# A 4096-cubed matmul on one core: the panel of B halved to 1024 columns and double-buffered, and the order of TensorE and of the loads written out by hand

## The chip, the cores and the metric

The kernel runs on one core of one Trainium2 chip. Times are device microseconds (us) of that core, from the start to the end of one execution; of several executions the median is given. The trace is of one profiled execution.

## The reference

```python
m, k, n = 4096, 4096, 4096
a = np.random.randn(m, k).astype(np.float32)
b = np.random.randn(k, n).astype(np.float32)
scale = np.float32(0.1)
out = np.matmul(a, b) * scale          # float32
```

The kernel multiplies in bf16 and sums in float32.

## The kernel before

All loads that change float32 into bf16 on the way (A and B) are issued by POOL, one DMA for 128 partitions x 512 columns: 256 KB are read from memory and 128 KB written to SBUF. All other DMAs (stores of the output, and the stores and loads of the transposed A) are issued by SP.

A comes in 32 row tiles `mt` of 128 rows. A is needed transposed, so `make_at` (lines 59 to 77) loads one row tile in eight DMAs into `arow_bf` (three buffers), transposes it on TensorE (PE) in 32 pieces into PSUM (line 72), and VectorE copies the result into `at` (line 73). Each `at` is also stored to a scratch tensor in memory, `at_dram` (line 75), from where `load_at` (lines 79 to 84) fetches it again for later columns.

B is held in SBUF by panels of `N_BLK` = 2048 columns: 32 slices of k (`ko`) times 4 column groups of 512, that is 128 tiles `bp` of 128 KB (line 119). The pool of `bp` has 136 slots (line 51). There are two panels, so two blocks `nb`: block 0 uses columns 0 to 2047 and makes every `at`; block 1 uses the other columns and loads every `at` again.

For one row tile, `matmuls` (lines 86 to 107) runs 128 matmuls of 128x128 by 128x512: two PSUM banks at a time, each of 32 steps of `ko` (line 93). ScalarE (ACT) multiplies the bank by the scale (line 103) and SP stores it (line 104).

The order of the instructions on each engine is set by the scheduler of the tile framework, with the order of the program as priority; each engine then runs its own queue in order. A DMA of POOL waits on its queue until the slot that it writes is free and until the DMA eight before it on the same queue has landed.

Of the kernel before, what the change touches and what calls it, by code (L numbers as in the profile page):

```python
# [1 line left out]

# [5 lines left out]

FP32 = mybir.dt.float32  # L10
BF16 = mybir.dt.bfloat16


@with_exitstack
def kernel(
    ctx: ExitStack,
    tc: tile.TileContext,
    a: bass.AP,
    b: bass.AP,
    scale: float,  # L20
    out: bass.AP,
):
    nc = tc.nc
    P = 128

    M, K = a.shape
    K2, N = b.shape
    assert K == K2

    N_BLK = 2048  # L30
    NT = 512
    KO = K // P
    MT = M // P
    PS_GRP = 2
    AROW_Q = 8
    AHEAD = 3

    n_blocks = N // N_BLK
    nts = N_BLK // NT

    b_r = b.rearrange("(ko ki) n -> ki ko n", ki=P)

    dram = ctx.enter_context(tc.tile_pool(name="dram", bufs=1, space=bass.MemoryType.DRAM))
    at_dram = dram.tile([MT, P, K], BF16)

    const_pool = ctx.enter_context(tc.tile_pool(name="const", bufs=1))
    ident = const_pool.tile([P, P], BF16)
    make_identity(nc, ident)

    arow_pool = ctx.enter_context(tc.tile_pool(name="arow", bufs=3))  # L50
    bp_pool = ctx.enter_context(tc.tile_pool(name="bp", bufs=KO * 4 + 8))
    at_pool = ctx.enter_context(tc.tile_pool(name="at", bufs=AHEAD + 1))
    cst_pool = ctx.enter_context(tc.tile_pool(name="cst", bufs=6))
    psum_pool = ctx.enter_context(tc.tile_pool(name="psum", bufs=2 * PS_GRP, space=bass.MemoryType.PSUM))
    psum_tr_pool = ctx.enter_context(tc.tile_pool(name="psum_tr", bufs=8 - 2 * PS_GRP, space=bass.MemoryType.PSUM))

    TRB = 8

    def make_at(mt):
        arow_bf = arow_pool.tile([P, K], BF16, tag="arow_bf")  # L60
        for q in range(AROW_Q):
            w = K // AROW_Q
            nc.gpsimd.dma_start(  # L63
                out=arow_bf[:, q * w:(q + 1) * w],
                in_=a[mt * P:(mt + 1) * P, q * w:(q + 1) * w],
            )
        at = at_pool.tile([P, KO, P], BF16, tag="at")
        for g in range(KO // TRB):
            ps_t = psum_tr_pool.tile([P, TRB, P], BF16, tag="pst", name="ps_t")
            for j in range(TRB):  # L70
                ko = g * TRB + j
                nc.tensor.transpose(ps_t[:, j], arow_bf[:, ko * P:(ko + 1) * P], ident)  # L72
            nc.vector.tensor_copy(out=at[:, g * TRB:(g + 1) * TRB, :], in_=ps_t)  # L73
        for q in range(2):
            nc.sync.dma_start(out=at_dram[mt, :, q * (K // 2):(q + 1) * (K // 2)],
                              in_=at[:, q * (KO // 2):(q + 1) * (KO // 2), :])
        return at

    def load_at(mt):
        at = at_pool.tile([P, KO, P], BF16, tag="at")  # L80
        for q in range(4):
            nc.sync.dma_start(out=at[:, q * (KO // 4):(q + 1) * (KO // 4), :],
                              in_=at_dram[mt, :, q * (K // 4):(q + 1) * (K // 4)])
        return at

    def matmuls(bp, at, mt, nb):
        for v in range(nts // PS_GRP):
            psums = [psum_pool.tile([P, NT], FP32, tag="ps", name="ps") for _ in range(PS_GRP)]
            for ko in range(KO):
                lhsT = at[:, ko, :]  # L90
                for g in range(PS_GRP):
                    nt = v * PS_GRP + g
                    nc.tensor.matmul(  # L93
                        psums[g],
                        lhsT,
                        bp[ko][nt],
                        start=(ko == 0),
                        stop=(ko == KO - 1),
                    )
            for g in range(PS_GRP):  # L100
                nt = v * PS_GRP + g
                cst = cst_pool.tile([P, NT], FP32, tag="cst")
                nc.scalar.mul(cst, psums[g], float(scale))  # L103
                nc.sync.dma_start(
                    out=out[mt * P:(mt + 1) * P, nb * N_BLK + nt * NT:nb * N_BLK + (nt + 1) * NT],
                    in_=cst,
                )

    at_q = []
    for nb in range(n_blocks):  # L110
        while len(at_q) < AHEAD:
            mt = len(at_q)
            at_q.append(make_at(mt) if nb == 0 else load_at(mt))

        bp = [[bp_pool.tile([P, NT], BF16, tag="bp", name="bp") for _ in range(nts)]
              for _ in range(KO)]
        for q in range(nts):
            for ko in range(KO):
                nc.gpsimd.dma_start(  # L119
                    out=bp[ko][q],  # L120
                    in_=b_r[:, ko, nb * N_BLK + q * NT:nb * N_BLK + (q + 1) * NT],
                )

        for mt in range(MT):
            at_cur = at_q.pop(0)
            if mt + AHEAD < MT:
                at_q.append(make_at(mt + AHEAD) if nb == 0 else load_at(mt + AHEAD))
            matmuls(bp, at_cur, mt, nb)
        at_q = []


# [1 line left out]
_INS = ['a', 'b', 'scale']  # L133
_OUTS = [((4096, 4096), 'float32')]
#: Inputs that are plain numbers.
_NUMBERS = {'scale': 0.10000000149011612}


# [26 lines left out]
```

## Time and profile before

| what | value |
|---|---|
| median of 4 runs | 1953.43 us (1952.56 to 1957.6) |
| the profiled execution's own time | 1957.6 us, the highest of the four |
| its span in the trace | 1955.8 us |
| PE busy | 1884.3 us, 96% of the span |
| matmuls on line 93 | 8192, of which 8017 have a record |
| transposes on line 72 | 1024 |
| mean granted clock of PE | 0.991 of full speed |
| mean DMA rate (bytes written) | 104 GB/s |

Ends of matmuls are modelled in this trace, so a busy PE isn't PE at its full rate; a few per cent of the matmul records are missing, while the weight loads (one for each matmul and each transpose, row PEld) are all there and count the work done. "Clock" is the clock of PE that was granted, 1.00 being 2.4 GHz and 0.50 being 1.2 GHz. "DMA share" is the busy time of the packets of the mean DMA engine over the stretch; packets of two queues overlap, so it goes above 1.

### The profile page before, as it was taken

What the parts mean: (1) busy time and instruction counts of PE and PEld (TensorE: products, weight loads), DVE (VectorE), ACT (ScalarE), POOL (GpSimd) and SP (SyncE); (2) the same over time, 40 slices, a digit from 0 to 9 for tenths busy, and PEclk for the clock granted to TensorE, in tenths of its full rate; (3) what the DMA queues carried; (4) which work ended last, traced back from release to release, by engine and by line L of the source; (5) the groups of instructions that cost most, each with busy time, mean ns of one, the idle gap of its engine ahead of it and who ended that gap; (6) DMA issues with size and microseconds to landing.
All of it is one profiled execution on the core that took longest, in us unless ns stands there. A gap on an engine that the chain in (4) does not pass through costs nothing.

```text
span 1955.8 us, 20456 instructions
## 1 busy us (share of the span) xinstructions
PE 1884.3 (96%) x9041; PEld 864.1 (44%) x9216; DVE 80.9 (4%) x128; ACT 140.5 (7%) x257; POOL 271.4 (14%) x518
## 2 busy tenths in 40 slices
PE   6889999999999999999996899999999999999999
PEld 2134444444444444444441344444444444444444
DVE  1011101101101101101000000000000000000000
ACT  0000000000000000000000000000000000000000
POOL 6762111111111111100036300000000000000000
PEclk9999999999999999999997999999999999999999
DMA  9997345345345345331269622222222122212201
GB/s 210 196 229 161 98 107 119 98 107 119 97 108 119 97 108 119 96 88 76 78 128 211 135 84 86 76 71 70 86 75 83 58 86 75 86 57 84 86 33 44
DMA packets 138328, 202.70 MB, mean 104 GB/s; under 512 B 15360, under 2 KB 80896, under 8 KB 138240
## 3 DMA queue, kind: packets, MB, share of 16 engines
q0 software_dynamic: 73728, 67.14, 22.5%
q1 hardware_dynamic: 64512, 134.25, 19.6%
q8 instruction: 72, 1.18, 0.3%
q14 instruction: 16, 0.13, 0.0%
HBM read 167.77 MB, written 100.66 MB: 137 GB/s over the span
## 4 chain that ended last, share of the span: by engine, by line
PE 88%; DMA 5%; issue 3%; POOL 3%; ACTq 0%; POOLq 0%; ACT 0%
PE ps L93 86%; DMA bp<-in_b_dram 4%; PE ps_t L72 3%; POOL bp L119 2%; DMA arow_bf<-in_a_dram 1%; POOL arow_bf L63 1%; ACTq L160 0%; POOL ident masks.py:199 0%; POOL ident masks.py:197 0%; ACT cst L103 0%; POOLq masks.py:199 0%; POOLq L119 0%; POOLq L160 0%; POOLq L146 0%
## 5 line engine op out<-in xcount | busy, mean ns | idle before, releaser
L93 PE MATMUL ps<-bp,at 128*128 128x512 bf16 x8017 | 1822.4, 383 | 49.3 <-DMA bp<-in_b_dram 31.7
L93 PEld LDWEIGHTS <-at 128*128 128x128 bf16 x8192 | 802.3, 98 | 1051.9 <-issue 103.3
L103 ACT ACTIVATE cst<-ps 128x512 f32<-128x512 f32 x256 | 139.2, 595 | 1811.4 <-issue 1658.4
L63 POOL DMA_DIRECT2D arow_bf<-in_a_dram x256 | 135.6, 560 | 597.8 <-PE ps_t L72 568.4
L119 POOL DMA_DIRECT2D bp<-in_b_dram x256 | 135.2, 532 | 225.6 <-PE ps L93 176.9
L73 DVE COPY at<-ps_t 128x1024 bf16<-128x1024 bf16 x128 | 80.9, 685 | 837.7 <-PE ps_t L72 837.7
L72 PE MATMUL ps_t<-ident,arow_bf 128*128 128x128 bf16 x1024 | 73.9, 229 | 18.1 <-DMA arow_bf<-in_a_dram 17.6
L72 PEld LDWEIGHTS <-arow_bf 128*128 128x128 bf16 x1024 | 63.6, 102 | 35.2 <-DMA arow_bf<-in_a_dram 28.0
L103 ACT ACT_TABLE_LOAD x1 | 1.3, 1283 | 0.7 <-PEq L146 0.7
masks.py:199 POOL TENSOR_SCALAR_AFFINE_SELECT ident<-ident 128x128 bf16<-128x128 bf16 x1 | 0.3, 304 | 0.1
masks.py:197 POOL MEMSET ident<- 128x128 bf16 x1 | 0.2, 204 | 0.3 <-POOLq L146 0.3
L146 POOL MEMSET const-float32-0.0<- 128x1 f32 x1 | 0.1, 99 | 0.2 <-issue 0.2
L146 POOL MEMSET const-bfloat16-1.0<- 128x1 bf16 x1 | 0.1, 102 | 0.0
L146 POOL MEMSET const-uint8-127<- 128x1 uint8 x1 | 0.1, 102 | 0.0
L146 POOL MEMSET const-float32-1.0<- 128x1 f32 x1 | 0.1, 99 | 0.0
## 6 DMA issues: line engine op xcount, KB each, us to landing
out_dram<-cst SPq DMA_DIRECT2D x256, 256.0 KB, 2.7
arow_bf<-in_a_dram POOLq DMA_DIRECT2D x256, 128.0 KB, 7.3
at_dram<-at SPq DMA_DIRECT2D x64, 512.0 KB, 6.3
bp<-in_b_dram POOLq DMA_DIRECT2D x256, 128.0 KB, 4.9
at<-at_dram SPq DMA_DIRECT2D x128, 256.0 KB, 5.0
```

Of the source, the lines that this page charges most:

```text
L63: nc.gpsimd.dma_start(out=arow_bf[:, q * w:(q + 1) * w], in_=a[mt * P:(mt + 1) * P, q * w:(q + 1) * w],)
L72: nc.tensor.transpose(ps_t[:, j], arow_bf[:, ko * P:(ko + 1) * P], ident)
L73: nc.vector.tensor_copy(out=at[:, g * TRB:(g + 1) * TRB, :], in_=ps_t)
L93: nc.tensor.matmul(psums[g], lhsT, bp[ko][nt], start=(ko == 0), stop=(ko == KO - 1),)
L103: nc.scalar.mul(cst, psums[g], float(scale))
L119: nc.gpsimd.dma_start(out=bp[ko][q], in_=b_r[:, ko, nb * N_BLK + q * NT:nb * N_BLK + (q + 1) * NT],)
L146: nc = _bacc.Bacc("TRN2", target_bir_lowering=False, num_devices=1)
```

## The change

A panel is 1024 columns wide, so there are four panels and four blocks; the pool of `bp` has 128 slots, two panels of 64. `make_at` now only issues the eight loads; the transposes, the copies and the stores to `at_dram` (now four DMAs of 256 KB where there were two of 512 KB) are in `transpose_at`. The queues of POOL and PE follow the order of the program (`manual_schedule`); the other engines are still scheduled by the framework. Blocks run through the row tiles up and down in turn, and the last four `at` of a block are kept for the start of the next, in a pool of five. The B loads of the next panel are issued in the second half of a block.

```diff
-    N_BLK = 2048
+    N_BLK = 1024
-    PS_GRP = 2
...
-    bp_pool = ctx.enter_context(tc.tile_pool(name="bp", bufs=KO * 4 + 8))
-    at_pool = ctx.enter_context(tc.tile_pool(name="at", bufs=AHEAD + 1))
+    bp_pool = ctx.enter_context(tc.tile_pool(name="bp", bufs=KO * nts * 2))
+    at_pool = ctx.enter_context(tc.tile_pool(name="at", bufs=AHEAD + 2))
...
+    def transpose_at(mt):
+        arow_bf = arows.pop(mt)
         at = at_pool.tile([P, KO, P], BF16, tag="at")
...
+    def mm(bp, mt, g):
+        ps = psum_pool.tile([P, NT], FP32, tag="ps", name="ps")
+        for ko in range(KO):
+            nc.tensor.matmul(ps, at_cache[mt][:, ko, :], bp[ko][g], start=(ko == 0), stop=(ko == KO - 1))
+        return ps
...
     def matmuls(bp, at, mt, nb):
...
+        psums = [psum_pool.tile([P, NT], FP32, tag="ps", name="ps") for _ in range(nts)]
+        for ko in range(KO):
+            for g in range(nts):
+                nc.tensor.matmul(psums[g], at[:, ko, :], bp[ko][g], start=(ko == 0), stop=(ko == KO - 1))
+        for g in range(nts):
+            evac(psums[g], mt, nb, g)
...
+    with tc.manual_schedule(engines={mybir.EngineType.Pool, mybir.EngineType.PE}):
+        make_at(0)
+        panels[0] = bp = alloc_panel()
+        for ko in range(KO):
+            b_chunk_load(bp, 0, ko, 0)
+        make_at(1)
+        make_at(2)
+        for ko in range(KO):
+            b_chunk_load(bp, 0, ko, 1)
+        for j in (3, 4, 5):
+            make_at(j)
+        transpose_at(0)
+        g0 = {0: mm(bp, 0, 0)}
+        transpose_at(1)
+        transpose_at(2)
+        g0[1] = mm(bp, 1, 0)
+        g0[2] = mm(bp, 2, 0)
+        for mt in range(3):
+            evac(g0[mt], mt, 0, 0)
+        for mt in range(3):
+            if mt == 2:
+                transpose_at(3)
+            evac(mm(bp, mt, 1), mt, 0, 1)
+
+        for nb in range(n_blocks):
+            order = list(range(MT) if nb % 2 == 0 else range(MT - 1, -1, -1))
+            bp = panels[nb]
+            next_jobs = []
+            if nb + 1 < n_blocks:
+                panels[nb + 1] = alloc_panel()
+                next_jobs = [(nb + 1, ko, q) for q in range(nts) for ko in range(KO)]
+            for i, mt in enumerate(order):
+                if nb == 0 and i < 3:
+                    del at_cache[mt]
+                    continue
+                if nb == 0:
+                    if i + 3 < MT:
+                        make_at(i + 3)
+                    if i + 1 < MT:
+                        transpose_at(i + 1)
+                else:
+                    for j in range(i + 1, min(i + 1 + AHEAD, MT)):
+                        if order[j] not in at_cache:
+                            load_at(order[j])
+                            break
+                if next_jobs and i >= MT // 2:
+                    k = (len(next_jobs) + (MT - i) - 1) // (MT - i)
+                    for _ in range(k):
+                        if next_jobs:
+                            b_chunk_load(panels[nb + 1], *next_jobs.pop(0))
+                matmuls(bp, at_cache[mt], mt, nb)
+                if i < MT - AHEAD - 1:
+                    del at_cache[mt]
+            keep = set(order[-(AHEAD + 1):])
...
```

POOL's queue before, from its first load to its end: `arow_bf` are pieces of A, `bp` pieces of B, `xN` how many stand in a row.

```order
L63 DMA arow_bf<-in_a_dram 128x512
masks.py:199 ISA
masks.py:199 AFFINE_SELECT ident<-ident 128x128
L63 DMA arow_bf<-in_a_dram 128x512 x23
L119 DMA bp<-in_b_dram 128x512 x128
L63 DMA arow_bf<-in_a_dram 128x512 x40
L119 DMA bp<-in_b_dram 128x512 x8
L63 DMA arow_bf<-in_a_dram 128x512 x192
L119 DMA bp<-in_b_dram 128x512 x120
```

POOL's queue now, at the same place:

```order
L64 DMA arow_bf<-in_a_dram 128x512 x7
L116 DMA bp<-in_b_dram 128x512 x32
L64 DMA arow_bf<-in_a_dram 128x512 x16
L116 DMA bp<-in_b_dram 128x512 x32
L64 DMA arow_bf<-in_a_dram 128x512 x136
L116 DMA bp<-in_b_dram 128x512 x4
L64 DMA arow_bf<-in_a_dram 128x512 x8
```

The first 24 pieces of A stood ahead of all 128 pieces of B; now 8 stand ahead of the first 32 of B and 16 more ahead of the other 32 of the first panel. The last two rows then alternate (twelve rows of four `bp` between rows of eight `arow_bf`), and the queue ends with 144 `bp` in a row: the last 16 pieces of panel 1 and all of panels 2 and 3.

PE's queue before, at the first matmul: `arow_bf_188` is the third row tile of A, `at_93` the first transposed one, the `bp` are pieces of B.

```order
L72 LDWEIGHTS arow_bf_188
L72 MATMUL ps_t_228<-ident_61,arow_bf_188 128x128
L93 LDWEIGHTS at_93
L93 MATMUL ps_548<-bp_240,at_93 128x512
L93 LDWEIGHTS at_93
```

PE's queue now, at the first matmul, and where the first column group of row tile 0 ends: `arow_bf_86` is the first row tile, `arow_bf_191` the second.

```order
L77 LDWEIGHTS arow_bf_86
L77 MATMUL ps_t_299<-ident_61,arow_bf_86 128x128
L96 LDWEIGHTS at_268
L96 MATMUL ps_313<-bp_95,at_268 128x512
...
L96 LDWEIGHTS at_268
L96 MATMUL ps_313<-bp_157,at_268 128x512
L77 LDWEIGHTS arow_bf_191
L77 MATMUL ps_t_347<-ident_61,arow_bf_191 128x128
```

The transposes of row tiles 1 and 2 moved behind the 32 matmuls of the first column group of row tile 0.

SP's queue now, at the start of block 1, for the second and third `at` that are loaded again there (`at_4587`, `at_4664`); `cst_4504` and `cst_4507` are the results of the block's first row tile, `cst_4581` of its second.

```order
L88 DMA at_4587<-at_dram_57 128x1024
L102 DMA out_0_dram<-cst_4504 128x512
L102 DMA out_0_dram<-cst_4507 128x512
L88 DMA at_4587<-at_dram_57 128x1024 x3
L88 DMA at_4664<-at_dram_57 128x1024
L102 DMA out_0_dram<-cst_4581 128x512
```

Between two pairs of stores stands one load of an `at`. `at_4587` is the block's sixth row tile and its slot comes free with the first, so it is issued about when the first row tile ends.

## Rows read from the trace of the kernel before

**Rows 1.** The page: span, and PE's busy tenths in 40 slices.

```profile
span 1955.8 us, 20456 instructions
PE   6889999999999999999996899999999999999999
```

**Rows 2.** Windows, line 93 (matmuls) alone: stretch, length, PE, PEld, clock, DMA share, GB/s.

```profile
0.00:136.26 136.26, 84.08 (x185) 20.15 (x190) 0.97 1.16 209
136.26:1015.03 878.77, 830.25 (x3760) 375.35 (x3849) 1.00 0.44 107
1015.03:1110.00 94.97, 70.44 (x252) 25.39 (x257) 0.86 1.09 195
1110.00:1951.50 841.50, 837.45 (x3822) 381.42 (x3898) 1.00 0.22 72
```

**Rows 3.** Windows, line 72 (transposes) alone, same columns.

```profile
0.00:136.26 136.26, 21.29 (x160) 13.14 (x160) 0.97 1.16 209
136.26:1015.03 878.77, 52.65 (x864) 50.50 (x864) 1.00 0.44 107
```

**Rows 4.** Windows, all engines: PE, PEld, DVE, ACT, POOL, clock, DMA share, GB/s.

```profile
500.00:600.00 100.00, 99.47 (x550) 49.27 (x559) 9.94 (x16) 7.60 (x14) 16.46 (x32) 1.00 0.45 112
1040.00:1060.00 20.00, 16.36 (x51) 5.13 (x51) 0.00 (x0) 1.08 (x2) 16.37 (x31) 0.91 1.21 202
1400.00:1600.00 200.00, 199.00 (x910) 90.65 (x927) 0.00 (x0) 15.31 (x29) 0.00 (x0) 1.00 0.25 82
```

**Rows 5.** The chain of waits: one row tile's transposes in the steady stretch (start, us).

```profile
150.88 1.79 PE ps_t L72 x32
```

**Rows 6.** Timeline at the end of the span: the last results scaled.

```profile
1951.56 1.08 ACT L103 ACTIVATE cst<-ps 128x512 f32<-128x512 f32 x2 [12.73 <-issue]
```

**Rows 7.** Timelines of POOL and PE at the change of block: start, us, work, [idle before].

```profile
1000.81 4.24 POOL L119 DMA_DIRECT2D bp<-in_b_dram  x8 [167.10 <-PE ps L93]
...
1078.28 5.90 PE L93 MATMUL ps<-bp,at 128*128 128x512 bf16 x19 [10.48 <-DMA bp<-in_b_dram]
```

**Rows 8.** Windows, line 93 alone, from the start to 72 us.

```profile
0.00:72.00 72.00, 35.97 (x63) 6.79 (x64) 1.00 1.15 209
```

**Rows 9.** Timeline of SP's issues in the first 116 us.

```profile
8.70 19.96 SPq L75 DMA_DIRECT2D at_dram<-at  x6
52.29 46.30 SPq L104 DMA_DIRECT2D out_dram<-cst  x3
```

**Rows 10.** Timeline: the first column group of row tile 0 scaled.

```profile
51.67 0.60 ACT L103 ACTIVATE cst<-ps 128x512 f32<-128x512 f32 x1 [49.64 <-PE ps L93]
```

**Rows 11.** Timeline of PE: the first and the last four transposes before the first matmul.

```profile
4.44 0.61 PE L72 MATMUL ps_t<-ident,arow_bf 128*128 128x128 bf16 x4 [4.44 <-DMA arow_bf<-in_a_dram]
...
26.98 0.61 PE L72 MATMUL ps_t<-ident,arow_bf 128*128 128x128 bf16 x4 [0.90 <-DMA arow_bf<-in_a_dram]
```

**Rows 12.** Windows, all engines, around 135 us, where the clock rises again.

```profile
130.00:135.00 5.00, 3.87 (x21) 2.31 (x22) 1.02 (x3) 0.00 (x0) 2.65 (x5) 0.50 1.17 245
135.00:140.00 5.00, 4.95 (x22) 2.21 (x22) 0.63 (x1) 1.08 (x2) 2.41 (x5) 0.93 1.19 244
```

**Rows 13.** Timeline of PE: the matmuls that follow there.

```profile
134.69 5.62 PE L93 MATMUL ps<-bp,at 128*128 128x512 bf16 x22
```

**Rows 14.** The page's DMA issues: count, KB each, us from issue to landing.

```profile
arow_bf<-in_a_dram POOLq DMA_DIRECT2D x256, 128.0 KB, 7.3
...
at<-at_dram SPq DMA_DIRECT2D x128, 256.0 KB, 5.0
```

**Rows 15.** DMAs that touch `at`, then the waits of the whole span for them.

```profile
DMA to landing us min/median/max: 2.8/5.0/10.4
...
PEld L93 <- DMA at<-at_dram: 1.0, 1, 1.0
```

More of the change, by code (lines that the diff above doesn't have):

```diff
@@ L33 @@
     MT = M // P
-    PS_GRP = 2
     AROW_Q = 8
     AHEAD = 3
+    TRB = 8
     n_blocks = N // N_BLK
@@ L66, in make_at @@
             )
+        arows[mt] = arow_bf
+    def transpose_at(mt):
+        arow_bf = arows.pop(mt)
         at = at_pool.tile([P, KO, P], BF16, tag="at")
@@ L73, in make_at @@
             nc.vector.tensor_copy(out=at[:, g * TRB:(g + 1) * TRB, :], in_=ps_t)
-        for q in range(2):
-            nc.sync.dma_start(out=at_dram[mt, :, q * (K // 2):(q + 1) * (K // 2)],
-                              in_=at[:, q * (KO // 2):(q + 1) * (KO // 2), :])
+        for q in range(4):
+            nc.sync.dma_start(out=at_dram[mt, :, q * (K // 4):(q + 1) * (K // 4)],
+                              in_=at[:, q * (KO // 4):(q + 1) * (KO // 4), :])
+        at_cache[mt] = at
         return at
@@ L83, in load_at @@
                               in_=at_dram[mt, :, q * (K // 4):(q + 1) * (K // 4)])
+        at_cache[mt] = at
         return at
-    def matmuls(bp, at, mt, nb):
[L87 to L129, printed above, removed]
+    def mm(bp, mt, g):
[3 more added lines that the diff above has]
+        return ps
@@ new lines, in evac @@
+    def evac(ps, mt, nb, g):
+        cst = cst_pool.tile([P, NT], FP32, tag="cst")
+        nc.scalar.mul(cst, ps, float(scale))
+        nc.sync.dma_start(
+            out=out[mt * P:(mt + 1) * P, nb * N_BLK + g * NT:nb * N_BLK + (g + 1) * NT],
+            in_=cst,
+        )
+    def matmuls(bp, at, mt, nb):
+        psums = [psum_pool.tile([P, NT], FP32, tag="ps", name="ps") for _ in range(nts)]
[4 more added lines that the diff above has]
+            evac(psums[g], mt, nb, g)
@@ new lines, in b_chunk_load, with alloc_panel @@
+    def b_chunk_load(bp, nb, ko, q):
+        nc.gpsimd.dma_start(
+            out=bp[ko][q],
+            in_=b_r[:, ko, nb * N_BLK + q * NT:nb * N_BLK + (q + 1) * NT],
+        )
+    def alloc_panel():
+        return [[bp_pool.tile([P, NT], BF16, tag="bp", name="bp") for _ in range(nts)]
+                for _ in range(KO)]
+    panels = [None] * n_blocks
+    with tc.manual_schedule(engines={mybir.EngineType.Pool, mybir.EngineType.PE}):
[51 more added lines that the diff above has]
+            keep = set(order[-(AHEAD + 1):])
+            for k in list(at_cache):
+                if k not in keep:
+                    del at_cache[k]
```

13 lines of the change are left out of this document (7 added, 6 removed).

## The prediction

> **What bounds the kernel now.** I read first the page: of a span of 1955.8 us PE is busy nearly throughout, with two weak places, the first three slices and the slices 22 and 23 of 48.9 us each [rows 1]. So the question is what PE loses there, and busy time can't answer it, since ends of matmuls are modelled. I therefore count weight loads (PEld), which are all recorded. In a stretch without stalls 927 matmuls start in 200 us, 0.2157 us each [rows 4], and the 32 transposes of a row tile take 1.79 us, 0.0559 us each [rows 5]. That makes a floor for this work of 8192 x 0.2157 + 1024 x 0.0559 = 1767.4 + 57.3 = 1824.7 us, which the change leaves as it is: it adds and removes no matmul and no transpose.
>
> Next I cut the span where the steady pattern begins and ends and set the work of each piece against its length [rows 2, 3]. From 0 to 136.26 us PE does 190 matmuls and 160 transposes, 41.0 + 8.9 = 49.9 us of work: 86.3 us are lost. From 136.26 to 1015.03: 3849 matmuls and 864 transposes are 878.5 us in 878.8: nothing lost. From 1015.03 to 1110.00, the change of block, 257 matmuls are 55.4 us: 39.5 us lost. From 1110.00 to 1951.5: 840.8 us of work, 0.7 lost. After the last matmul 4.3 us pass, with the last scaling [rows 6] and its store. Floor and losses together are 1955.5 us of the 1955.8.
>
> What PE waits for in both places is B. At the change of block POOL had been held for 167.1 us, because its next load needed a slot that a matmul still read; then it issues one panel, and PE sits idle for up to 10.5 us at a time for pieces of it [rows 7]. While only POOL's loads run, 31 pieces land in 20 us, one per 0.645 us; they write 202 GB/s and, as float32 is read for bf16 written, read twice that [rows 4]. I take 0.645 us as the price of any DMA that reads 256 KB, whoever issues it. It holds in the steady stretch: a row tile there has 8 loads of A, 4 units of stores to at_dram and 4 output stores, 16 x 0.645 = 10.3 us in the 128 x 0.2157 + 1.79 = 29.4 us between two row tiles, 35%; the row shows a share of 0.45 where the saturated one shows 1.21, 37% [rows 4].
>
> **The change of block goes.** With 128 slots for two panels of 64 pieces, panel 1 needs no slot of panel 0. Its pieces stand in POOL's queue in fours behind the loads of row tiles 19 to 30, and the last sixteen behind the loads of row tile 31. The loads of a row tile wait for a buffer that comes free with the transposes three row tiles earlier, so the last of panel 1 is issued some three row tiles before block 0 ends; a row tile of block 0 is now 64 x 0.2157 + 1.79 = 15.6 us, so over 40 us ahead against some 13 us for twenty pieces. Panels 2 and 3 are issued in one burst each when the panel before last is freed, 64 x 0.645 = 41 us, a whole block (32 x 13.8 = 442 us) before they are read. Nothing but later B loads is queued behind POOL's wait then. So 39.5 us go, three times over nothing is late in their place, and there is no fourth such wait.
>
> **The start shrinks.** Before, all 128 pieces of the wide panel had to land behind 24 of A. Now the first 88 DMAs of POOL are 8 of A, 32 of B, 16 of A, 32 of B, and after them PE has all of panel 0. The same set of 88 (24 of A and 64 of B) has a row: the 64th matmul, which waits for the 64th piece of B, has begun by 72.0 us [rows 8]. The stores in the same time are the same too, at_dram for three row tiles and about two outputs [rows 9]. So the last piece lands at about 72.0 us, whatever their order, and the fourth group of 32 matmuls ends at 72.3. The other way round, PE's own path must not be later: piece 56 (the third row tile of A) landed by 51 us, where 32 matmuls were through [rows 10], behind 12 units of at_dram of which 8 now come later: 51 - 8 x 0.645 = 46 us; then 64 matmuls, 13.8 us, to 60; the fourth group waits for B, not for PE. At 72.3 us PE will have done 128 matmuls and 96 transposes, 27.6 + 5.4 = 33.0 us of work: 39.3 us lost. Then PE goes from waiting to dense work. In the trace the clock was 0.50 just before such a place and 0.93 on average after it [rows 12], and 22 matmuls took 5.62 us [rows 13] in place of 4.75, 0.9 us more. I add 1.0: 40.3 us lost in place of 86.3, a gain of 46.0.
>
> Bounds of this term. If the stores cost POOL's loads nothing, PE's path decides: 46 + 13.8 + 1 + 6.9 = 67.7 us for the end of the fourth group, and a gain of 51.6. If the 88 pieces come at the pace of the first 24, from 4.44 to 26.98 us [rows 11], 0.98 us each, the last lands at 4.4 + 87 x 0.98 = 89.7 and the gain is 28. I take 46.0, as rows 8 has the same set of transfers.
>
> The Trainium skill, HBM Reference, Specifications and Access, gives a core about 358 GB/s while its neighbour streams too, and about 425 alone. By the first a piece would take 0.73 us, the start would lose some 9 us more and the time would be 1877 us; by the second 0.62. The row at 0.645 [rows 4] is near the second, as one core runs here.
>
> **Edits at nothing, and their cover.** Block 0 has the same loads of A in about half the time. In its second half a row tile asks for 8 + 4 loads, 4 units of at_dram and 2 output stores: 18 x 0.645 = 11.6 us in 15.6. The load of A is asked for three row tiles (47 us) ahead and lands in 7.3 us [rows 14]. Loads of `at` rise from 32 to 84 row tiles, each 4 DMAs of 256 KB: with 2 stores 6 x 0.645 = 3.9 us in 13.8. Each is asked for more than 30 us ahead, a slot of five being free with the row tile before, and landed in 5.0 us, at most 10.4 [rows 14, 15]; in the one burst of B that the trace has, PE waited for `at` once, for 1.0 us [rows 15]. On SP's queue the store of a result stands behind the first DMA of an `at`, which waits for the same row tile. If that cover went, each `at` could cost up to 5.0 us. ScalarE has two scalings per 13.8 us, 1.08 us [rows 6], with two PSUM banks to spare. The end stays at 4.3.
>
> **The sum.** 1955.8 - 39.5 - 46.0 = 1870.3 us of span. Outside the span the profiled execution had 1957.6 - 1955.8 = 1.8 us, so 1872.1. It was the slowest of four, 4.2 above the median of 1953.43; against the median that is 1868 us.
>
> **The rivals.**
> First, block 0 becomes bound by DMA. It decides above 15.6 / 18 = 0.87 us per unit. For it: the first 24 pieces came at 0.98 [rows 11]. Then sixteen row tiles take 17.6 in place of 15.6 us, 32 us more: 1900. Against it: at_dram's stores ran beside those 24 [rows 9] and account for the difference.
> Second, the next panel comes late all the same, because POOL stands at a wait of A when panel 1 is due: the one stall of 39.5 us stays, 1907 us. For it: POOL's queue is now in the order of the program; against it the lead above.
> Third, the clock. In the paced transposes the clock fell to 0.50 [rows 12]. If each of the 28 later blocks of transposes now did that to the 64 matmuls behind it, 28 x 0.9 = 25 us: 1893. Against it: with 864 transposes in blocks of 32 the clock stayed at 1.00 [rows 3]. The Trainium skill, TensorE: Matmul & The Clock Gate, Part 4, says that transposes don't count as busy to the clock gate; by that rule this rival would be more likely, as their share doubles, and the trace shows no sign of it yet.
> Fourth, and slower: the new wait is for `at`. If each of the 84 loads came late by more than 85.5 / 84 = 1.02 us, the gain is gone; with the whole 5.0 us exposed it is 1868 + 420 = 2288 us. It needs the lead of some 30 us to be lost, by the slots or by SP's order.
>
> **How the numbers follow.** The forecast of 1868 has 0.81, DMA in block 0 0.08, the clock 0.04, the late panel 0.03, `at` late 0.04. The bounds of the start alone give 1862 to 1886; with a few us less or more elsewhere and the third rival the range is 1855 to 1896, which leaves about 2 in 10 out. A difference under 0.2% (4 us) can't be told from none here. All but the last rival are faster; of it 0.01 lies near no change: faster 0.96, same 0.01, slower 0.03.
>
> **What would show it.** In the profile after: the last piece of panel 0 lands near 72 us and 128 matmuls are begun by then; from about 75 us to the end weight loads come at the steady rate, with no wait for `bp` and no weak slice at any of the three changes of block; POOL waits for long on slots, and nobody for it. The span is about 1870. Wrong would be: waits for `arow_bf` in the second half of block 0, a wait for `at` repeated in blocks 1 to 3, the clock at 0.50 after transposes, or a last piece of panel 0 at 85 us and later.

## The result and the profile after

The changed kernel takes 1875.1 us (median of 8 runs, 1874.08 to 1877.67) against 1955.09 us for the kernel before (13 runs in all, 1952.56 to 1958.72): a ratio of 0.9591 with a 95% interval of 0.9582 to 0.9601. The profiled execution took 1874.23 us, and its span is 1872.4 us.

The page shows the span and PE's busy tenths in 40 slices; both weak places of [rows 1] are to be looked for.

```profile
span 1872.4 us, 20875 instructions
PE   6999999999999999999999999999999999999999
```

Only the first slice is weak now. As before, busy time doesn't say how much is lost; counts of weight loads do. These are windows of single lines (stretch, length, PE, PEld, clock, DMA share, GB/s), line 77 the transposes:

```profile
0.00:75.40 75.40, 14.59 (x96) 8.27 (x96) 1.00 1.14 208
75.40:93.28 17.88, 3.73 (x64) 3.74 (x64) 1.00 1.19 237
93.28:540.00 446.72, 52.81 (x867) 50.51 (x864) 1.00 0.87 186
```

then line 96, the matmuls of the hand-written start:

```profile
0.00:75.40 75.40, 40.35 (x125) 13.41 (x128) 1.00 1.14 208
75.40:93.28 17.88, 14.42 (x64) 6.20 (x64) 1.00 1.19 237
```

and line 111, the matmuls of the loop:

```profile
93.28:540.00 446.72, 400.19 (x1796) 179.55 (x1848) 1.00 0.87 186
540.00:1868.10 1328.10, 1321.67 (x6033) 602.00 (x6153) 1.00 0.40 116
```

With the prices of the kernel before, 0.2157 us for a matmul and 0.0559 for a transpose, the table reads like [rows 2, 3]: up to 93.28 us PE does 192 matmuls and 160 transposes, 50.4 us of work, so 42.9 us are lost, where 86.3 were. From 93.28 to 1868.1 us 8000 matmuls (one weight load more falls into two windows) and 864 transposes are 1773.9 us in 1774.8: under 1 us lost over three changes of block. The end, 4.3 us from the last matmul, is as before [rows 6]:

```profile
1868.22 1.08 ACT L101 ACTIVATE cst<-ps 128x512 f32<-128x512 f32 x2 [12.73 <-issue]
```

Around the first change of block PE runs at its rate while POOL issues panel 2 (windows of all engines, columns as in [rows 4]):

```profile
500.00:540.00 40.00, 39.74 (x206) 19.13 (x210) 2.71 (x5) 2.17 (x4) 7.80 (x15) 1.00 0.56 142
540.00:600.00 60.00, 59.74 (x275) 27.18 (x279) 0.00 (x0) 5.43 (x10) 25.98 (x50) 1.00 1.02 208
```

279 weight loads in 60 us are 0.215 us each, beside 50 loads of B. At the same kind of place PE had stood idle for up to 10.5 us [rows 7]. The waits of the whole span say who waits now:

```profile
POOL bp L116 <- PE ps L111: 438.4, 13, 385.5
...
POOL arow_bf L64 <- PE ps_t L77: 196.9, 24, 11.4
...
PE ps L96 <- DMA bp<-in_b_dram: 4.9, 9, 1.0
```

POOL waits long for slots, and nobody waits for POOL; PE waits for `bp` in the start alone. This is the start on PE (timeline: start, us, work, [idle before]):

```profile
12.96 1.26 PE L96 MATMUL ps<-bp,at 128*128 128x512 bf16 x2 [0.44 <-DMA bp<-in_b_dram]
...
26.33 9.69 PE L96 MATMUL ps<-bp,at 128*128 128x512 bf16 x15 [0.17 <-DMA bp<-in_b_dram]
36.13 6.42 PE L77 MATMUL ps_t<-ident,arow_bf 128*128 128x128 bf16 x40
...
52.27 21.74 PE L96 MATMUL ps<-bp,at 128*128 128x512 bf16 x91 [0.22 <-issue]
...
75.19 7.77 PE L96 MATMUL ps<-bp,at 128*128 128x512 bf16 x33 [0.43 <-DMA bp<-in_b_dram]
```

The first 32 matmuls go one by one with the pieces of B (15 in 9.69 us), the transposes with the pieces of A. From 52.27 us on PE runs nearly without a wait: only at 74.38 and 75.19, with the last matmuls of the fourth group, does it wait for B. The ends of the groups can be read from ScalarE, which scales each as it ends; these are the second, third and fourth:

```profile
60.86 0.60 ACT L101 ACTIVATE cst<-ps 128x512 f32<-128x512 f32 x1 [24.21 <-PE ps L96]
67.77 0.60 ACT L101 ACTIVATE cst<-ps 128x512 f32<-128x512 f32 x1 [6.31 <-PE ps L96]
76.10 0.60 ACT L101 ACTIVATE cst<-ps 128x512 f32<-128x512 f32 x1 [7.73 <-PE ps L96]
```

The fourth group ends at about 75.9 us, 6.9 us before the next 32 matmuls are through at 82.80.

### The profile page after: what moved, and what is told of

It reads as the page before. It is cut to its first block, busy times and chain, and to the rows that moved or that the text cites. A ratio compares the mean times of both kernels' runs of the same rounds, so it can differ in the third digit from the quotient of the medians.

```text
span 1872.4 us, 20875 instructions
## 1 busy us (share of the span) xinstructions
PE 1838.6 (98%) x9039; PEld 862.4 (46%) x9216; DVE 80.4 (4%) x128; ACT 140.5 (8%) x257; POOL 271.3 (14%) x518
## 3 DMA queue, kind: packets, MB, share of 16 engines
q0 software_dynamic: 73728, 67.14, 23.5%
## 5 line engine op out<-in xcount | busy, mean ns | idle before, releaser
L111 PE MATMUL ps<-bp,at 128*128 128x512 bf16 x7827 | 1722.1, 379 | 9.1
L96 PE MATMUL ps<-bp,at 128*128 128x512 bf16 x188 | 54.8, 426 | 6.7 <-DMA bp<-in_b_dram 4.9
L96 PEld LDWEIGHTS <-at 128*128 128x128 bf16 x192 | 19.6, 103 | 40.4 <-issue 23.4
```

Of the source, the lines that this page charges most:

```text
L96: nc.tensor.matmul(ps, at_cache[mt][:, ko, :], bp[ko][g], start=(ko == 0), stop=(ko == KO - 1))
L111: nc.tensor.matmul(psums[g], at[:, ko, :], bp[ko][g], start=(ko == 0), stop=(ko == KO - 1))
```

## The experiments

Theory T: the start is bound by DMA, at one price per byte read, whoever issues it and in whatever size and order, and what PE can do by then is set by how many matmuls each landed piece of B allows; two panels of slots take the stall at the change of block away. The rivals are named with each run. "Lost" is the span less the floor of 1824.7 us and the end of 4.3; the changed kernel has 43.4. Ratios are to the kernel before.

**The order of the loads alone.** The three row tiles of A first, as before the change; PE's order as after it.

```diff
         make_at(0)
+        make_at(1)
+        make_at(2)
         panels[0] = bp = alloc_panel()
         for ko in range(KO):
             b_chunk_load(bp, 0, ko, 0)
-        make_at(1)
-        make_at(2)
         for ko in range(KO):
             b_chunk_load(bp, 0, ko, 1)
```

> The changed kernel with the loads of its first panel in the order of the kernel before: 24 pieces of A, then 64 of B; the order on TensorE is the changed one. Theory T (the start is set by the whole set of transfers that must land before panel 0 is complete, in any order): the 88th piece lands at about 75.5 us as in the changed kernel, TensorE has done 128 matmuls and 96 transposes then, 1875 us, within 2. Rival O (the order of the loads made the gain at the start): TensorE starts its first matmul some 15 us later and that is not caught up, 1885 us or more.

Measured: 1875.51 us, ratio 0.9592 (0.9579 to 0.9605), span 1873.3. PE's timeline:

```profile
25.53 20.76 PE L96 MATMUL ps<-bp,at 128*128 128x512 bf16 x32 [13.39 <-DMA bp<-in_b_dram]
...
74.89 8.97 PE L96 MATMUL ps<-bp,at 128*128 128x512 bf16 x33 [0.28 <-DMA bp<-in_b_dram]
```

The first matmul starts at 25.5 instead of 13.0 us and the last waits for its piece at 74.9 instead of 75.2. The order of the loads gained nothing: rival O falls. The narrower first panel and PE's new order are left, and no run takes these two apart.

**Half as many, larger loads of B.**

```diff
...
+        if ko % 2:
+            return
         nc.gpsimd.dma_start(
-            out=bp[ko][q],
-            in_=b_r[:, ko, nb * N_BLK + q * NT:nb * N_BLK + (q + 1) * NT],
+            out=pairs[nb][ko // 2][q],
+            in_=b_r[:, ko:ko + 2, nb * N_BLK + q * NT:nb * N_BLK + (q + 1) * NT],
         )
...
```

> The changed kernel with B loaded in pieces of twice the size (two slices of k per DMA, 512 KB read), half as many DMAs. Theory T (bytes through the DMA engines set the pace of POOL's loads): the pace per byte stays, panel 0 is complete at about 75 us, 1875 us, within 2. Rival I (POOL's issue sets it: 0.53 us busy for a DMA whatever its size): the 64 pieces of panel 0 cost half as much, TensorE's own path binds, 1866 to 1869 us.

Measured: 1874.46 us, ratio 0.9579 (0.9565 to 0.9593). One window of all engines in the start, first of the changed kernel, then of this one:

```profile
20.00:30.00 10.00, 9.13 (x17) 1.90 (x17) 0.00 (x0) 0.00 (x0) 8.63 (x17) 1.00 1.22 194
```

```profile
20.00:30.00 10.00, 7.50 (x15) 2.02 (x16) 0.00 (x0) 0.00 (x0) 5.13 (x8) 1.00 1.24 204
```

Eight loads of 512 KB in 10 us write 204 GB/s, 17 of 256 KB wrote 194. The pace belongs to the bytes. POOL is busy 5.1 us in place of 8.6 and it changes nothing: rival I falls.

**The stores of the first row tiles later.** SP's queue follows the program in this one, and the three stores to at_dram stand behind the start.

```diff
-    with tc.manual_schedule(engines={mybir.EngineType.Pool, mybir.EngineType.PE}):
+    with tc.manual_schedule(engines={mybir.EngineType.Pool, mybir.EngineType.PE, mybir.EngineType.SP}):
...
             evac(mm(bp, mt, 1), mt, 0, 1)
+        for mt in range(3):
+            store_at(mt, at_cache[mt])
```

> The changed kernel with the stores to at_dram of the first three row tiles moved behind the last result of the hand-written start, with SP's queue too in the order of the program. Theory T (every DMA costs the start 0.645 us per 256 KB read, whoever issues it): 12 units fewer before the last piece of panel 0, which lands at about 68 us; there TensorE's own path binds, so 5 to 7 us gained, 1869 us. Rival I (the issue of POOL, 0.53 us busy per DMA and a gap, sets the pace and stores of SP cost its loads nothing): the last piece lands at about 75 us as before, 1875 us.

Measured: 1865.33 us, ratio 0.954 (0.9527 to 0.9553), span 1863.6, 34.6 lost.

```profile
12.00 20.71 PE L100 MATMUL ps<-bp,at 128*128 128x512 bf16 x32
...
43.81 22.52 PE L100 MATMUL ps<-bp,at 128*128 128x512 bf16 x95
66.80 7.28 PE L100 MATMUL ps<-bp,at 128*128 128x512 bf16 x33 [0.47 <-DMA bp<-in_b_dram]
```

The last piece of panel 0 is waited for at 66.8 in place of 75.2 us: 8.4 us for 12 stores of 256 KB, 0.70 us each. I had taken 0.645 and thought that PE's own path would then bind at 68; A landed sooner too (the second group starts at 43.8 us, in the changed kernel at 52.3, and I had the third row tile of A at 46), so the gain was 10 us and not 5 to 7.

The control, with SP's order alone and no store moved (only the first two lines of the diff):

> The changed kernel with SP's queue too in the order of the program, nothing else: the control for the late stores, which had both edits. Theory T (moving the stores gained those 10 us): 1875 us, within 2. Rival Q (SP's order did): 1865 us.

Measured: 1874.63 us, ratio 0.9584 (0.957 to 0.9597). So the stores made it, not SP's order.

**Four matmuls for each piece.** Four row tiles of A first; then PE does one matmul of each of them per piece of B.

```diff
...
+        for g in range(nts):
+            g4 = [psum_pool.tile([P, NT], FP32, tag="ps", name="ps") for _ in range(4)]
+            for ko in range(KO):
+                for mt in range(4):
+                    nc.tensor.matmul(g4[mt], at_cache[mt][:, ko, :], bp[ko][g], start=(ko == 0), stop=(ko == KO - 1))
+            for mt in range(4):
+                evac(g4[mt], mt, 0, g)
```

> Loads: four row tiles of A, then the 64 pieces of panel 0; TensorE then does four matmuls (one for each of the four row tiles) for each piece of B. Theory T (at the start TensorE lacks work for each piece that lands): A is there at about 34 us, 256 matmuls follow at 0.2157 us without waiting for B, 55 us, so at about 91 us 256 matmuls and 128 transposes are done, 62.4 us of work; lost 28 us in place of 42.6, 1861 us. Rival C (the clock stays at its lower level while matmuls are paced by loads): the 256 matmuls take up to 110 us and nothing is gained or up to 40 us lost, 1875 to 1915 us.

Measured: 1865.66 us, ratio 0.9543 (0.953 to 0.9556), span 1863.8, 34.8 lost.

```profile
38.14 58.61 PE L142 MATMUL ps<-bp,at 128*128 128x512 bf16 x256 [1.26 <-DMA bp<-in_b_dram]
96.59 3.79 PE L77 MATMUL ps_t<-ident,arow_bf 128*128 128x128 bf16 x64
```

PE doesn't wait for B any more, and the clock isn't the limit: 256 matmuls in 58.6 us, so rival C falls. But they start at 38.1 and not at 34, behind 32 pieces of A and 16 stores, and they took 3.4 us more than 256 x 0.2157; 2.1 of these went at the beginning, where 13 weight loads took from 38.14 to 43.00 us. A gain of 10 where 14 was expected.

**Both.**

> Both: four row tiles of A first with four matmuls for each piece of B, and the first four row tiles' stores to at_dram moved behind the hand-written start. Theory T: the 32 pieces of A are there at about 26 us instead of 34, 256 matmuls end at about 83 us, 62.4 us of work done, lost 20 to 21 us in place of 42.6: 1853 us. Rival I (stores cost the loads nothing): as with four matmuls per piece alone, 1861 us.

Measured: 1861.25 us, ratio 0.952 (0.9507 to 0.9533), span 1859.8, 30.8 lost.

```profile
28.28 57.63 PE L146 MATMUL ps<-bp,at 128*128 128x512 bf16 x256
85.75 3.79 PE L82 MATMUL ps_t<-ident,arow_bf 128*128 128x128 bf16 x64
...
107.75 3.57 PE L82 MATMUL ps_t<-ident,arow_bf 128*128 128x128 bf16 x32 [4.40 <-DVE at L83]
```

The time is the 1861 us of rival I, but the trace isn't: the matmuls start at 28.28 us and not at 38.14, so the stores do cost the loads. At 85.75 us 62.4 us of work are done, 23.4 lost, near the 20 to 21 expected. The rest is a new wait at 103 us: the transposes stood 4.40 us, as the copies of the sixth row tile wait for a slot that the late store of the first still read; then 32 transposes took 3.57 us, not 1.79, with the clock at 0.50. A stall had only been moved. The wait of the copies, and the window of those transposes (all engines):

```profile
DVE at L83 <- DMA at_dram<-at: 21.1, 2, 18.1
```

```profile
107.75:111.11 3.36, 3.36 (x32) 3.36 (x32) 1.74 (x3) 0.00 (x0) 0.00 (x0) 0.50 1.14 286
```

**Three, then four.**

```diff
+        for mt in range(3):
+            transpose_at(mt, False)
+        group([0, 1, 2], 0)
+        transpose_at(3, False)
+        group([3], 0)
+        for mt in range(4):
+            store_at(mt, at_cache[mt])
+        group([0, 1, 2, 3], 1)
+        transpose_at(4)
```

> A start built on theory T: three row tiles of A, the first 32 pieces of B with three matmuls each (0.647 us of work for a piece that lands every 0.645 us), the fourth row tile of A, then the other 32 pieces with four matmuls each; the stores to at_dram of these four behind the results of the first column group. T: 24 pieces at about 20.5 us, the first group ends at about 42, the fourth row tile at about 55, the rest 28 us later, at about 83 us with 62.4 us of work done: 20 to 21 us lost in place of 42.6, 1852 us. Rival S (as with four row tiles first, something beside DMA holds the start at some 30 us lost): 1861 us.

Measured: 1869.96 us, ratio 0.9554 (0.954 to 0.9568), span 1867.9, 38.9 lost: worse than both numbers. PE's timeline, then two windows of all engines:

```profile
49.87 31.22 PE L147 MATMUL ps<-bp,at 128*128 128x512 bf16 x141
81.75 1.85 PE L147 MATMUL ps<-bp,at 128*128 128x512 bf16 x7 [0.66 <-DMA bp<-in_b_dram]
...
100.94 0.60 PE L82 MATMUL ps_t<-ident,arow_bf 128*128 128x128 bf16 x4 [1.21 <-DMA arow_bf<-in_a_dram]
```

```profile
60.00:70.00 10.00, 9.95 (x47) 4.55 (x47) 0.00 (x0) 0.00 (x0) 4.73 (x9) 1.00 1.14 290
...
90.00:100.00 10.00, 3.83 (x28) 2.16 (x28) 2.30 (x4) 0.00 (x0) 3.84 (x8) 0.62 1.14 287
```

My count was at fault, and by T's own price: I had left the 16 stores and 4 outputs, 13 us of DMA, out of the stretch from 46 to 85 us. They run there (POOL gets 9 loads in 10 us instead of 16), B's last pieces come late, and the fifth and sixth row tiles of A still later: PE crawls through their transposes to 102 us, with the clock at 0.62 between 90 and 100. The greater part is lost there: by 85.95 us the 62.4 us of work were done, 23.5 lost, 3 us behind the 83 that I had.

**The slot given back in time.** As with four row tiles and late stores, but the first store behind the results of the first column group.

```diff
                 evac(g4[mt], mt, 0, g)
+            if g == 0:
+                store_at(0, at_cache[0])
...
-        for mt in range(4):
+        for mt in range(1, 4):
             store_at(mt, at_cache[mt])
```

> The kernel with four row tiles first and late stores, in which TensorE then stood for 4.4 us at 103 us, since the slot of the sixth transposed row tile waited for the late store of the first. Here that one store goes out behind the results of the first column group, the other three stay late. Theory T (256 KB read cost 0.645 us, and the window from 57 to 85 us has room for 4 units more): the start stays at 23 to 24 us lost by its end, the 4.4 us stall and the slow transposes behind it go, 1854 us, within 2. Rival M (the store pushes the next loads of A behind the end of the start, as with three then four matmuls per piece): 1861 us or more.

Measured: 1855.09 us, ratio 0.9484 (0.9471 to 0.9497), span 1853.7, 24.7 lost.

```profile
29.37 57.25 PE L146 MATMUL ps<-bp,at 128*128 128x512 bf16 x256
86.45 3.79 PE L82 MATMUL ps_t<-ident,arow_bf 128*128 128x128 bf16 x64
...
103.90 1.95 PE L82 MATMUL ps_t<-ident,arow_bf 128*128 128x128 bf16 x32
```

The stall at 103 us is gone and PE runs on. This version beats both kernels: 5.2% below the kernel before, 20 us below the changed one.

**One panel of slots.** The double buffer undone; the next panel's loads stand behind those of the block.

```diff
-    bp_pool = ctx.enter_context(tc.tile_pool(name="bp", bufs=KO * nts * 2))
+    bp_pool = ctx.enter_context(tc.tile_pool(name="bp", bufs=KO * nts))
...
-                if next_jobs and i >= MT // 2:
...
+            if next_jobs:
+                panels[nb + 1] = alloc_panel()
+                for job in next_jobs:
+                    b_chunk_load(panels[nb + 1], *job)
```

> The changed kernel with slots for one panel (64) in place of two, the loads of the next panel standing behind those of the block: the double buffer is undone, the narrow panel and the start are kept. Theory T (two panels of slots are what took the stall at the change of block away): each of the three changes now waits for 64 pieces, 41 us, from the start of the last row tile (13.8 us) on; the last lands some 30 us after the block's end, while 13.8 us of work wait for it: 17 to 18 us lost three times, 1925 to 1932 us. Rival N (the hand-written start and the order of the row tiles made the gain): 1875 us. Rival W (a change costs what the wide one cost): 3 x 39.5, 1993 us.

Measured: 1943.49 us, ratio 0.9929 (0.9914 to 0.9944), span 1941.9, so 69.5 us more than the changed kernel, 23.2 for each of three changes. The first of them on PE, and the waits of the whole span:

```profile
534.75 8.36 PE L111 MATMUL ps<-bp,at 128*128 128x512 bf16 x37
558.57 12.06 PE L111 MATMUL ps<-bp,at 128*128 128x512 bf16 x37 [15.45 <-DMA bp<-in_b_dram]
```

```profile
PE ps L111 <- DMA bp<-in_b_dram: 48.7, 7, 15.9
PEld L111 <- DMA bp<-in_b_dram: 47.6, 3, 16.3
```

T's mechanism holds, its size was 5 us short for each change; where these 5 us go wasn't tried. Rivals N and W fall. Without the second panel of slots four narrow panels give back most of what the change gains, 69.5 of 83.4 us of span.

**The lead of `at`.**

```diff
-    AHEAD = 3
+    AHEAD = 1
```

> The changed kernel with the transposed row tiles asked for one row tile ahead instead of three and three slots for them instead of five (two, not four, are kept over a change of block). Theory T (a row tile is there 5 us, at most some 10 us, after its issue, and 13.8 us are enough): 1875 us, within 2. Rival A (these loads are late as soon as the lead is one row tile): 90 loads late by 1 us or more, 1965 us or more; late only beside the burst of B at the start of a block: four row tiles twice, up to 30 us, 1905 us.

Measured: 1875.1 us, ratio 0.9581 (0.9565 to 0.9597). No wait for `at` appears. But the edit did less than I had meant: the framework orders SP's queue, and a load goes out as soon as its slot is free. These are the last three DMAs of the last `at` of the span, first in the changed kernel, then here:

```profile
1800.65 1.60 SPq L88 DMA_DIRECT2D at<-at_dram  x3
```

```profile
1828.53 1.61 SPq L88 DMA_DIRECT2D at<-at_dram  x3
```

The row tile that needs them starts at 1854.4 us in both, so the lead fell from 54 to 26 us, and not to 13.8. Half of the lead is enough; rival A at a lead of one row tile wasn't tried. The DMAs of `at` (stores and loads) landed as here, first the changed kernel, then this one:

```profile
DMA to landing us min/median/max: 2.6/5.2/11.9
```

```profile
DMA to landing us min/median/max: 2.6/5.1/11.1
```

## Why the prediction was right

**The change of block**: 39.5 us were to go and nothing was to be late in their place. From 93.28 us on under 1 us is lost, and with one panel of slots the stall is back. Right, in mechanism and size.

**The start**: a gain of 46.0 was predicted, 43.4 came (86.3 to 42.9). That the transfers set when panel 0 is there is shown from three sides: neither the order nor the size of the loads is worth anything, and with 12 stores taken out the last piece is waited for 8.4 us earlier. More matmuls for each piece shorten the loss. Two terms were mis-sized.

The first is the last piece of panel 0, put at 72.0 us. That was read from the 64 weight loads of [rows 8], but a weight load can run before the piece of B that its matmul waits for has landed, and the same row counts 63 matmuls. The group of 32 that ends with the 64th matmul was scaled at 73.19 us in the kernel before:

```profile
73.19 0.60 ACT L103 ACTIVATE cst<-ps 128x512 f32<-128x512 f32 x1 [20.92 <-PE ps L93]
```

Here the fourth group, which needs the same set of pieces, is scaled at 76.10. Of these 2.9 us two output stores may be 1.4, at the 0.70 measured: the kernel before had issued one by 72.4 us, this one three by 75.2, where I had about two in both. The rest is open.

The second is PE's own path, put at 60 us before the fourth group. The third row tile of A was through at 52.3 us and not at 46, the second group then took 8.6 us where the third took 6.9, and the third was scaled at 67.77. The fourth, with its two waits, took 8.3. So B held PE up for only 1.4 us, and with the last piece at 72.0 the group would still have ended at about 74.5, not 72.3. That "the fourth group waits for B, not for PE" came out by a narrow margin, and that this term is off by no more than 2.6 us is in part luck: the piece came late enough to hide most of PE's path. The 1.0 us added for the clock was lost in the second group rather than behind the fourth: its first 9 weight loads took from 52.27 to 55.70 us, but the 32 matmuls behind the fourth took 6.9 us, their result being scaled at 83.00.

The runs don't separate the narrower panel from PE's new order. At 72.0 us the kernel before had done 64 matmuls and 96 transposes, 19.2 us of work; with a panel that is complete there and the old order about 53 us would be lost, an estimate from [rows 8, 11], and PE's new order puts 64 more matmuls into that time. The wide panel with the new order wasn't tried.

**At nothing**: loads of A in block 0, 84 loads of `at` instead of 32, twice the scalings per time. Right: no such wait is in the trace, and half of the lead is enough for `at`.

**The sum**: a span of 1870.3 was predicted and 1872.4 came. The median is further off, 1875.1 for 1868, as I had taken 4.2 us off because the profiled execution of before was the slowest of four. With more runs of the kernel before its median is 1955.09, 2.5 under that execution, and the changed kernel's profiled execution lies 0.9 under its own median. The correction was noise of four runs.

**The rivals**: block 0 bound by DMA: its share of DMA is 0.87 from 93 to 540 us, against 1.2 where DMA is the bound, and PE loses nothing there. (The share goes above 1 with one queue too, not only where two overlap: POOL's alone took 1.17 from 1040 to 1060 us of the kernel before.) The late panel: no. The clock: it stayed at 1.00 with 864 transposes in twice the density; by the Trainium skill's page TensorE: Matmul & The Clock Gate, Part 4, where transposes don't count as busy in the same way, this was the likelier, and the trace shows no loss by it. `at` late, the slower one: its lead could be halved.

## What to carry to other kernels

Count a start in bytes that must land before the loop is fed, stores included, and in work that each landed piece allows; the order of the loads matters little while both stay the same. A double buffer made by halving the tile is worth its price when the smaller tile's other costs (here 2.6 times the reloads) lie beside work with time to spare. When a transfer is put off, look for the slot that it holds and for the loads that it meets later: twice here the gain came back as a wait some 20 us on.

## What of the hardware I had not expected

In the start of both kernels the clock's row says 1.00, but single matmuls paced by loads take 0.58 us there, near the 0.63 of the kernel before in its stretch at 0.50 [rows 12], and not the 0.38 of the steady stretch. Timelines of PE, first of the kernel before in that stretch, then of the changed kernel's start:

```profile
130.78 0.63 PE L93 MATMUL ps<-bp,at 128*128 128x512 bf16 x1
```

```profile
14.54 0.58 PE L96 MATMUL ps<-bp,at 128*128 128x512 bf16 x1 [0.32 <-DMA bp<-in_b_dram]
...
74.38 0.38 PE L96 MATMUL ps<-bp,at 128*128 128x512 bf16 x1 [0.37 <-DMA bp<-in_b_dram]
```

The run with SP's order alone settles it. Its PE does the same work in the same 14 us of the start as the changed kernel's (57 and 56 weight loads, 8.49 and 8.54 us busy), but its row shows 0.50 there; windows of all engines, first of the changed kernel, then of that run:

```profile
36.00:50.00 14.00, 8.54 (x57) 4.83 (x56) 4.84 (x7) 0.60 (x1) 7.59 (x15) 1.00 1.18 251
```

```profile
36.00:50.00 14.00, 8.49 (x59) 4.79 (x57) 4.84 (x7) 0.33 (x1) 7.39 (x15) 0.50 1.20 242
```

Four transposes in a row take 0.61 us in both. So in these starts the durations tell the clock, and the row does not.
